# Narrow expert tiles: gate and up in four column groups, on branches of TensorE alone

## The chip, the cores and the metric

One core of a Trainium2 chip runs the whole kernel. The metric is the time of one execution on the device in microseconds; the time before is a median of 3 runs.

## The reference, cut to what matters

One decoder layer over 512 tokens of width 1024: a mixer (a Mamba-2 branch and a forgetting-attention branch between two large projections) and then a hierarchical mixture of 16 experts. The change touches the experts alone:

```python
def hierarchical_moe(h, w_rg, b_rg, w_re, b_re, w_gate, w_up, w_down):
    ...
    gates = (onehot_g[:, :, None] * w_group[:, None, :]).reshape(-1, N_EXPERTS).astype(t.dtype)
    out = jnp.zeros_like(t)
    for e in range(N_EXPERTS):
        hid = jax.nn.silu(t @ w_gate[e]) * (t @ w_up[e])
        out = out + gates[:, e:e + 1] * (hid @ w_down[e])
    return out.reshape(b, s, d)
```

Each token picks one group of four experts and two experts in it, so only two of its 16 gates are not zero. `w_gate` and `w_up` are 1024 x 512 for each expert, `w_down` 512 x 1024, all float32. With the inputs given, experts 0 to 15 get 31, 40, 95, 86, 27, 11, 40, 32, 91, 132, 170, 103, 25, 21, 59 and 61 tokens.

## The kernel before, in words

The mixer and the router fill the time up to about 576 us. Then, for each expert `e`, tokens are taken in tiles of `H` = 64 slots: `body(e, 0)` always, `body(e, 1)` under `tc.If(n_toks[e] > H)` (L1354) and `body(e, 2)` nested in it under `tc.If(n_toks[e] > 2 * H)` (L1356). With the counts above that makes 24 tiles. After the sixteen experts stand ten nested overflow blocks `over(t)` (from L1421), none of which runs with these inputs: all engines jump over them.

A tile goes through these steps. `tile_ranks` and `tile_tokens` (VectorE comparisons L1151, small TensorE matmuls L1156 and L1158, then a gather by GpSimd, L1161) make the list of the tile's tokens, two experts ahead, and fetch their rows; `x_columns` (L1181, four transposes) turns the rows; `up` (L1283 to 1289, matmul L1288) multiplies by gate and up; `hidden` (L1292, L1293) forms silu(gate) * up; `hidden_columns` (four transposes L1297, copy L1298) turns it; `down` (L1303) multiplies it by `w_down` one tile later; `add` (L1307, L1308) weighs the rows and scatter-adds them to memory.

In `up` the 64 tokens are the stationary side (128 x 64 weights of the array) and 512 columns of the expert's weights stream past. Gate goes to rows 0 to 63 of the PSUM bank, up to rows 64 to 127, eight steps of k each:

```python
for k in range(KT):
    for n, w in enumerate(strm.up(e, k)):
        nc.tensor.matmul(bank[n * H:(n + 1) * H], xT[:, ...], w, start=(k == 0), stop=(k == KT - 1))
```

A float32 matmul shows as two weight loads and two matmul records in the trace. Weights come in pieces of 1 MB on SyncE's queue into at least 18 buffers (`Experts.load`, `drop`, L355 to 376), some three experts' worth.

The order of TensorE, VectorE and ScalarE inside a body is the written one (`in_order`); around the bodies the scheduler places instructions itself, and moves some over an `If`. For a branch each engine loads the expert's count into a register (`values_load`, L1347; the load stands just ahead of the branch on all engines but SyncE, which loads all 16 at once) and its sequencer then compares and jumps over the code of the bodies that don't run.

Of the kernel before, what the change touches and what calls it, by code (L numbers as in the profile page):

```python
# [9 lines left out]
F32 = mybir.dt.float32  # L10
F32R = mybir.dt.float32r
BF16 = mybir.dt.bfloat16
I32 = mybir.dt.int32
# [4 lines left out]
P = 128  # L18
S = 512
D = 1024  # L20
NT = S // P
KT = D // P
FF = 512
NE = 16
# [4 lines left out]
UNIT = 512  # L29
EVAC = 400  # L30
DUE = 8, 4, 4
H = P // 2
INL = 3
MAXO = 10

# [72 lines left out]
def hybrid_layer(ctx: ExitStack, tc: tile.TileContext, A, out):  # L108
    nc = tc.nc

    cp = ctx.enter_context(tc.tile_pool(name="cp", bufs=1))
# [57 lines left out]
    ident = cp.tile([P, P], F32, name="ident")  # L169
# [67 lines left out]
    class Stream:  # L237
# [7 lines left out]
        def add(self, units, loads, parts):  # L245
            for n, part in enumerate(parts):
                self.parts.append((len(self.raws), n == len(parts) - 1) + part)
            self.raws.append((units, loads))
# [96 lines left out]
    class Experts:  # L345
# [18 lines left out]
        def up(self, e, k):  # L364

            assert self.nload >= 6 * e + 4
            return [self.piece(6 * e + 2 * (k // 4) + n)[:, k % 4 * FF:(k % 4 + 1) * FF] for n in range(2)]

        def down(self, e, k):
            assert self.nload >= 6 * e + 6  # L370
            return [self.piece(6 * e + 4 + k // 2)[:, k % 2 * D + n * 512:k % 2 * D + (n + 1) * 512]
                    for n in range(2)]
# [5 lines left out]
    ew = Experts([(wg_all[e], wu_all[e], wd_all[e]) for e in range(NE)], [])  # L378
# [25 lines left out]
    for j in range(4):  # L404
# [14 lines left out]
        for t, sc_ in enumerate((1, 0)):  # L419
            o = 8 * sc_ + 2 * j  # L420
# [142 lines left out]
    for g in range(4):  # L563
# [17 lines left out]
        for c in range(NT):  # L581
            nc.tensor.matmul(pt[:, c * P:(c + 1) * P], Bc.ap[:, c * P:(c + 1) * P], Cc.ap[:, c * P:(c + 1) * P],
                             start=True, stop=True)
# [14 lines left out]
        for c2 in range(2):  # L598
            pt = tr.get()
            for c in (2 * c2, 2 * c2 + 1):  # L600
                for t in range(2):
                    o = (c % 2) * 256 + t * P
# [96 lines left out]
    for j in range(4):  # L699
# [22 lines left out]
        for i in range(NT):  # L722
            w = (i + 1) * P
# [36 lines left out]
        o = FM.alloc(1)  # L760
# [81 lines left out]
    for j in range(8):  # L842
        for y in (ys[j], ya[j]):
            pt = proj(hT, KT)
            t = FM.alloc(1)
# [18 lines left out]
    def rtile(nm, shape, dt=F32):  # L864
        if dt is I32:
            return cp.tile(shape, dt, name=f"rt_{nm}")
        n = 1
        for d in shape[1:]:
            n *= d
        w = n if dt is F32 else -(-n // 2)  # L870
        a = rtc[0][:, rtc[1]:rtc[1] + w]
        if dt is not F32:
            a = a.bitcast(dt)[:, 0:n]
        rtc[1] += -(-w // 2) * 2
        for ax_ in range(len(shape) - 1, 1, -1):
            a = a.rearrange("p (a b) -> p a b", b=shape[ax_]) if ax_ == len(shape) - 1 else \
                a.rearrange("p (a b) c -> p a b c", b=shape[ax_])
        return a
# [8 lines left out]
    half = rtile("half", [P, 1])  # L887
    nc.vector.tensor_scalar(half, pcol, float(H), None, op0=ALU.is_ge)
    nc.vector.tensor_scalar(itb[:, 0:H], itf[:, 0:H], 1.0, None, op0=ALU.add)
    nc.vector.tensor_copy(itb[:, H:P], itb[:, 0:H])  # L890
    itbs = [itb] + [rtile(f"itb{t}", [P, P], BF16) for t in range(1, INL)]
    for t in range(1, INL):
        nc.vector.tensor_scalar(itbs[t], itb, float(t * H), None, op0=ALU.add)
    aux = rtile("aux", [P, NT, NE, 5], BF16)
# [82 lines left out]
    @contextmanager  # L977
    def in_order(engines):

        traced = nc.cur_bb.bb.instructions  # L980
        n, prev = len(traced), {}
        yield
        for ins in traced[n:]:
            if ins.engine in engines:
                if ins.engine in prev:
                    tc.add_manual_dep(ins, prev[ins.engine], mybir.DependencyInfo(
                        mybir.DependencyClass.NoSync, mybir.DependencyReason.DATA), reason="in_order")
                prev[ins.engine] = ins.name
# [60 lines left out]
    ET = mybir.EngineType  # L1049
# [60 lines left out]
    bgu, bys, bhid, bix = (banks[0], banks[1], banks[1]), [banks[2], banks[6]], banks[5], banks[7]  # L1110
    h2d2 = h2d.rearrange("s (h d) -> (s h) d", h=2)
    moed2 = moed.rearrange("s (h d) -> (s h) d", h=2)
    xgs, xTs, sgs, yos, ohs = {}, {}, [], [], []
# [12 lines left out]
    def setup_experts():  # L1126
# [6 lines left out]
        yos.extend(FM.alloc(1).ap for _ in range(2))  # L1133
        hidT.append(FM.alloc(1).v(4, H))
        for _ in range(3):
# [4 lines left out]
        ew.raws.append(xrc[1].ap)  # L1140
        ew.load()

    ixs = [[rtile(f"ix{e}{t}", [P, 1], I32) for t in range(INL)] for e in range(3)]
    gws = [[rtile(f"gw{e}{t}", [P, 1]) for t in range(INL)] for e in range(3)]
    ixl = [rtile(f"ixl{e}", [P, 1], I32) for e in range(2)]
    gwl = [rtile(f"gwl{e}", [P, 1]) for e in range(2)]
    rkx = rtile("rkx", [P, NT])

    def onehots(oh, ranks, slots):
# [3 lines left out]
    def tokens(oh, au, ix, gw, xg, n0=0, n1=5, at=128):  # L1153

        pi = bix[:, at + n0:at + n1]
        nc.tensor.matmul(pi, onesb, bigb[:, n0:n1], start=True, stop=False)  # L1156
        for c in range(NT):
            nc.tensor.matmul(pi, oh[:, c, :], au(c)[:, n0:n1], start=False, stop=(c == NT - 1))  # L1158
        if n0 == 0:
            nc.vector.tensor_scalar(ix, bix[:, at:at + 1], bix[:, at + 1:at + 2], half, op0=ALU.add, op1=ALU.add)  # L1160
            nc.gpsimd.indirect_dma_start(out=xg, out_offset=None, in_=h2d2,  # L1161
                                         in_offset=bass.IndirectOffsetOnAxis(ap=ix[:, 0:1], axis=0),
                                         bounds_check=2 * S - 1, oob_is_err=False)
        if n1 == 5:
            nc.vector.tensor_reduce(gw, bix[:, at + 2:at + 5], axis=AX.X, op=ALU.add)  # L1165

    def oh_of(e, t):
        return ohs[t if e or t == 2 else 3 + t]

    def tile_ranks(e, t):  # L1170
        onehots(oh_of(e, t), rk[:, :, e], itbs[t])

    def tile_tokens(e, t, n0=0, n1=5):
        tokens(oh_of(e, t), lambda c: aux[:, c, e, :], ixs[e % 3][t], gws[e % 3][t], xgs[e % 2, t], n0, n1,
               128 + 8 * (e % 2 * 3 + t))

    def x_columns(xg, xT):

        pt = tr.get()
        for b in range(4):  # L1180
            nc.tensor.transpose(pt[:, b * P:(b + 1) * P], xg[:, b * P:(b + 1) * P], ident)  # L1181
        nc.scalar.copy(xT, pt)  # L1182
# [21 lines left out]

    NB = S // H - INL
    cnt = rtile("cnt", [P, 16])
    cnti = rtile("cnti", [P, 17], I32)
# [20 lines left out]
    with in_order((ET.PE, ET.DVE, ET.Activation)):  # L1228
# [46 lines left out]
        for e, t in early:  # L1275
            tile_ranks(e, t)
            tile_tokens(e, t, 0, 2)
# [7 lines left out]
    def up(strm, e, xT, bank):  # L1285
        for k in range(KT):
            for n, w in enumerate(strm.up(e, k)):
                nc.tensor.matmul(bank[n * H:(n + 1) * H], xT[:, (2 * (k % 4) + k // 4) * H:(2 * (k % 4) + k // 4 + 1) * H],  # L1288
                                 w, start=(k == 0), stop=(k == KT - 1))

    def hidden(bank, sg):
        nc.scalar.activation(sg[H:P], bank[0:H], AF.Silu)  # L1292
        nc.vector.tensor_tensor(sg[H:P], sg[H:P], bank[H:P], op=ALU.mult)  # L1293

    def hidden_columns(sg):
        for t in range(4):
            nc.tensor.transpose(bhid[:, t * P:(t + 1) * P], sg[:, t * P:(t + 1) * P], ident)  # L1297
        nc.vector.tensor_copy(hidT[0], bhid.rearrange("p (k s) -> p k s", s=P)[:, :, H:P])  # L1298

    def down(strm, e, bank):  # L1300
# [11 lines left out]
    def body(e, t):  # L1312

        bank, by, yo, sg = bgu[t], bys[t % 2], yos[t % 2], sgs[t % 2]
        with in_order((ET.PE, ET.DVE, ET.Activation)):
            if t == 0:
                if e + 2 < NE:
                    for u in range(2):
                        tile_ranks(e + 2, u)
                tile_ranks(e, 2)  # L1320
            if t == 1:
                tile_tokens(e, 2)
            up(ew, e, xTs[e % 2, t], bank)
            if e == 0 and t == 0:
                for e_, t_ in early:
                    tile_tokens(e_, t_, 2, 5)
            hidden(bank, sg)
            nc.vector.tensor_copy(ixl[e % 2], ixs[e % 3][t])
            nc.vector.tensor_copy(gwl[e % 2], gws[e % 3][t])
            if t:  # L1330
                down(ew, e, by)
                add(by, yo, ixs[e % 3][t - 1], gws[e % 3][t - 1])
            elif e:
                down(ew, e - 1, by)
                add(by, yo, ixl[1 - e % 2], gwl[1 - e % 2])
                ew.drop(2)
            if t == 0 and e + 1 < NE:
                for u in range(2):
                    x_columns(xgs[1 - e % 2, u], xTs[1 - e % 2, u])
            if t == 1:  # L1340
                x_columns(xgs[e % 2, 2], xTs[e % 2, 2])
            hidden_columns(sg)
            if t == 0 and e + 2 < NE:
                for u in range(2):
                    tile_tokens(e + 2, u)

    n_toks = [nc.values_load(cnti[0:1, e:e + 1], min_val=0, max_val=S) for e in range(NE)]  # L1347
    n_over = nc.values_load(cnti[0:1, 16:17], min_val=0, max_val=MAXO)
    n_raw = len(ew.raws)
    assert n_raw >= 18  # L1350

# [6 lines left out]
        if e + 1 < NE:  # L1358
            ew.drop(4)
    down(ew, NE - 1, bys[0])  # L1360
    add(bys[0], yos[0], ixl[(NE - 1) % 2], gwl[(NE - 1) % 2])


    spare = [ew.piece(6 * (NE - 3) + n) for n in range(18)]
# [103 lines left out]
```

## Time and profile before

| what | value |
|---|---|
| median of 3 runs | 932.13 us (930.22 to 933.62) |
| the profiled execution's own time | 932.47 us |
| span of its trace | 930.6 us |
| mean granted clock of TensorE | 0.964 |
| TensorE busy | 842.8 us, 91% of the span |
| VectorE, ScalarE, GpSimd busy | 540.6, 309.6, 101.3 us |
| moved by the DMA engines | 194.88 MB, mean 209 GB/s |

The profile counts an engine as busy while a matmul, a copy or the like runs; register loads, branches and waits of the engine's sequencer are not in it, but they have rows of their own (engine names with a q at the end, as PEldq for TensorE's sequencer). [...] The share of DMA can come out a little over 1 in a short window.

### The profile page before, as it was taken

What the parts mean: (1) busy time and instruction counts of PE and PEld (TensorE: products, weight loads), DVE (VectorE), ACT (ScalarE), POOL (GpSimd) and SP (SyncE); (2) the same over time, 40 slices, a digit from 0 to 9 for tenths busy, and PEclk for the clock granted to TensorE, in tenths of its full rate; (3) what the DMA queues carried; (4) which work ended last, traced back from release to release, by engine and by line L of the source; (5) the groups of instructions that cost most, each with busy time, mean ns of one, the idle gap of its engine ahead of it and who ended that gap; (6) DMA issues with size and microseconds to landing.
All of it is one profiled execution on the core that took longest, in us unless ns stands there. A gap on an engine that the chain in (4) does not pass through costs nothing. (4 is left out here: it accounts for less than half of the span.)

```text
span 930.6 us, 11855 instructions
## 1 busy us (share of the span) xinstructions
PE 842.8 (91%) x4216; PEld 542.3 (58%) x4216; DVE 540.6 (58%) x1310; ACT 309.6 (33%) x558; POOL 101.3 (11%) x113
## 2 busy tenths in 40 slices
PE   2899989999999999999999995999999999999850
PEld 1678768887666677878888883433343333333320
DVE  6849879858876687977745784423333223122216
ACT  5438788444643432432233451101110010001100
POOL 1001000000000000000000011122222221122210
PEclk9899999999999999999999985999999999999985
DMA  9951457213122248795445289598799998459734
GB/s 288 340 147 52 152 173 191 87 40 103 46 69 72 91 140 268 222 302 160 147 143 186 106 305 398 211 385 296 247 391 386 385 381 287 145 192 314 278 71 180
DMA packets 137170, 194.88 MB, mean 209 GB/s; under 512 B 11819, under 2 KB 85723, under 8 KB 137073
## 3 DMA queue, kind: packets, MB, share of 16 engines
q1 hardware_dynamic: 127040, 174.81, 55.3%
q0 software_dynamic: 9584, 18.45, 7.6%
q8 instruction: 46, 0.75, 0.3%
q10 hardware_dynamic: 464, 0.58, 0.2%
q14 instruction: 36, 0.29, 0.1%
HBM read 189.04 MB, written 13.16 MB: 217 GB/s over the span
## 5 line engine op out<-in xcount | busy, mean ns | idle before, releaser
L398 PE MATMUL bank<-rm,rm 128*128 128x512 f32 x512 | 206.2, 407 | 0.4 <-ACT rm L431 0.4
L400 PE MATMUL bank<-rm,rm 128*128 128x512 f32 x512 | 205.8, 402 | 0.0
L399 PE MATMUL bank<-rm,rm 128*128 128x512 f32 x512 | 204.8, 400 | 0.2 <-DVE rm L433 0.2
L1288 PE MATMUL bank<-fm,fm 128*64 128x512 f32 x408 | 123.8, 601 | 4.4 <-issue 2.0
L1288 PE MATMUL bank<-bm,fm 128*64 128x512 f32 x360 | 118.4, 597 | 1.6 <-PEq L1356 0.4
L234 DVE TENSOR_TENSOR rm<-fm,rm 128x1024 fp32r<-128x1024 f32 (+1 forms) x76 | 87.6, 1163 | 42.9 <-ACT rm L233 27.3
L398 PEld LDWEIGHTS bank<-rm,rm 128*128 128x128 f32 x512 | 97.8, 192 | 21.9 <-issue 3.1
L399 PEld LDWEIGHTS bank<-rm,rm 128*128 128x128 f32 x512 | 97.4, 190 | 21.5 <-issue 2.1
L400 PEld LDWEIGHTS bank<-rm,rm 128*128 128x128 f32 x512 | 97.1, 190 | 20.8 <-issue 2.3
L1293 DVE TENSOR_TENSOR bm<-bm,bank 64x512 f32<-64x512 f32 x24 | 16.6, 692 | 152.4 <-ACT bm L1292 143.4
L233 ACT CAST rm<-fm 128x1024 fp32r<-128x1024 f32 (+1 forms) x76 | 75.2, 1007 | 79.5 <-PE bank L399 59.5
L1292 ACT ACTIVATE bm<-bank 64x512 f32<-64x512 f32 x24 | 14.1, 588 | 198.8 <-PE bank L1288 198.8
L1288 PEld LDWEIGHTS bank<-fm,fm 128*64 128x64 f32 x408 | 37.9, 138 | 59.3 <-issue 58.4
L1303 PE MATMUL bank<-bm,fm 128*64 128x512 f32 x256 | 65.2, 593 | 0.7 <-DVEq L1354 0.7
L1288 PEld LDWEIGHTS bank<-bm,fm 128*64 128x64 f32 x360 | 34.7, 137 | 47.7 <-issue 46.8
L390 DVE SCALAR_TENSOR_TENSOR fm<-fm,cact,fm 128x256 f32<-128x256 f32 x112 | 51.2, 480 | 1.8
L1182 ACT COPY fm<-bank 128x512 f32<-128x512 f32 x38 | 20.9, 588 | 85.8 <-PE bank L1181 85.7
L1307 DVE SCALAR_TENSOR_TENSOR fm<-bank,fm,fm 128x512 f32<-128x512 f32 x24 | 18.0, 750 | 47.8 <-PE bank L1303 42.8
L1001 PE MATMUL bank<-rm,rm 128*128 128x512 f32 x192 | 44.2, 391 | 0.3 <-ACT fm L846 0.3
L1161 POOL DMA_INDIRECT bm<-h2d,rt_ix x38 | 39.0, 1027 | 38.9 <-DVE fm L1165 18.2
L1303 PEld LDWEIGHTS bank<-bm,fm 128*64 128x64 f32 x256 | 22.1, 137 | 35.3 <-issue 34.4
L1308 POOL DMA_INDIRECT moed<-fm,rt_ixl x16 | 25.5, 1596 | 152.2 <-DVE fm L1307 152.2
(314 smaller groups left out, 1101.7 us busy)
## 6 DMA issues: line engine op xcount, KB each, us to landing
bm<-in_w_down SPq DMA_DIRECT2D x22, 1024.0 KB
fm<-in_w_in SPq DMA_DIRECT2D x36, 512.0 KB
fm<-in_w_gate SPq DMA_DIRECT2D x17, 1024.0 KB
fm<-in_w_mod SPq DMA_DIRECT2D x16, 1024.0 KB
fm<-in_w_up SPq DMA_DIRECT2D x16, 1024.0 KB
bm<-in_w_up SPq DMA_DIRECT2D x16, 1024.0 KB
bm<-in_w_gate SPq DMA_DIRECT2D x15, 1024.0 KB
fm<-in_w_down SPq DMA_DIRECT2D x10, 1024.0 KB
```

The lines of the kernel that those rows point to most:

```text
L233: ins = nc.scalar.copy(hi, src)
L234: nc.vector.tensor_tensor(lo, src, hi.bitcast(F32), op=ALU.subtract)
L390: nc.vector.scalar_tensor_tensor(acc, r, cact[:, k:k + 1], acc, op0=ALU.mult, op1=ALU.add)
L398: nc.tensor.matmul(pt, whi[:, k, :], ah.ap, start=(k == 0), stop=False)
L399: nc.tensor.matmul(pt, whi[:, k, :], al.ap, start=False, stop=False)
L400: nc.tensor.matmul(pt, wlo[:, k, :], ah.ap, start=False, stop=(k == nk - 1))
L1001: nc.tensor.matmul(wps[i][hf], sta.ap[:, tsl], mov.ap[:, hf * 512:(hf + 1) * 512], start=(k == 0 and sta is mh and mov is wh), stop=(k == ...
L1161: nc.gpsimd.indirect_dma_start(out=xg, out_offset=None, in_=h2d2, in_offset=bass.IndirectOffsetOnAxis(ap=ix[:, 0:1], axis=0), bounds_check ...
L1182: nc.scalar.copy(xT, pt)
L1288: nc.tensor.matmul(bank[n * H:(n + 1) * H], xT[:, (2 * (k % 4) + k // 4) * H:(2 * (k % 4) + k // 4 + 1) * H], w, start=(k == 0), stop=(k = ...
L1303: nc.tensor.matmul(bank[n * H:(n + 1) * H], hidT[0][:, k, :], w, start=(k == 0), stop=(k == 3))
L1308: nc.gpsimd.indirect_dma_start(out=moed2, in_=yo, in_offset=None, compute_op=ALU.add, out_offset=bass.IndirectOffsetOnAxis(ap=ix[:, 0:1], ...
```

## The change

Expert tiles with at most `Q` = 32 tokens take another form of two steps. `up_few` uses only 32 of the 64 stationary columns, and splits gate and up by halves of their 512 columns: four blocks of 32 rows of the bank, each with 256 columns, 32 matmuls of 128 x 32 by 256 in place of 16 of 128 x 64 by 512. `turn_few` follows that layout: four float32 matmuls against 32 columns of the identity in place of four transposes. `by_width` chooses at run time, by an `If` and `Else` on TensorE alone, from a count that is loaded on TensorE (`n_pe`). Tiles (0, 0) and (0, 2) keep the old form without a branch. With the inputs given nine tiles hold at most 32 tokens and have the branch: the first tiles of e4, e5, e7, e12 and e13, the second of e2, e3 and e8, the third of e9. The lists of slots and gate weights (`ixs`, `gws`, `ixl`, `gwl`) become slices of one tile each, with a place of its own for every expert instead of two or three that are used in turn.

```diff
-H = P // 2
+H, Q = P // 2, P // 4
...
-    ixs = [[rtile(f"ix{e}{t}", [P, 1], I32) for t in range(INL)] for e in range(3)]
-    gws = [[rtile(f"gw{e}{t}", [P, 1]) for t in range(INL)] for e in range(3)]
-    ixl = [rtile(f"ixl{e}", [P, 1], I32) for e in range(2)]
-    gwl = [rtile(f"gwl{e}", [P, 1]) for e in range(2)]
+
+    ixa, gwa = cp.tile([P, NE, INL + 1], I32, name="ixa"), cp.tile([P, NE, INL + 1], F32, name="gwa")
+    ixs, gws = ([[a[:, e, t:t + 1] for t in range(INL)] for e in range(NE)] for a in (ixa, gwa))
+    ixl, gwl = ([a[:, e, INL:INL + 1] for e in range(NE)] for a in (ixa, gwa))
...
-        tokens(oh_of(e, t), lambda c: aux[:, c, e, :], ixs[e % 3][t], gws[e % 3][t], xgs[e % 2, t], n0, n1,
+        tokens(oh_of(e, t), lambda c: aux[:, c, e, :], ixs[e][t], gws[e][t], xgs[e % 2, t], n0, n1,
...
+    def up_few(strm, e, xT, bank):
+        for k in range(KT):
+            at = (2 * (k % 4) + k // 4) * H
+            for n, w in enumerate(strm.up(e, k)):
+                for hf in range(2):
+                    o = n * H + hf * Q
+                    nc.tensor.matmul(bank[o:o + Q, 0:256], xT[:, at:at + Q], w[:, hf * 256:(hf + 1) * 256],
+                                     start=(k == 0), stop=(k == KT - 1), tile_position=(0, o))
...
-    def hidden_columns(sg):
+    def by_width(is_few, few, other, *args):
+        if is_few is None:
+            return other(*args)
+        with tc.If(is_few) as arm:
+            with in_order((ET.PE,)):
+                few(*args)
+        with arm.Else():
+            with in_order((ET.PE,)):
+                other(*args)
+
+    def turn_few(sg):
+        for t in range(4):
+            o = H + t // 2 * Q
+            nc.tensor.matmul(bhid[:, t * P + H:t * P + H + Q], sg[:, t % 2 * P:(t % 2 + 1) * P], ident[:, o:o + Q],
+                             start=True, stop=True)
+
+    def turn(sg):
         for t in range(4):
             nc.tensor.transpose(bhid[:, t * P:(t + 1) * P], sg[:, t * P:(t + 1) * P], ident)
+
+    def hidden_columns(sg, is_few=None):
+        by_width(is_few, turn_few, turn, sg)
...
+        is_few = None if (e, t) in wide else n_pe[e] <= t * H + Q
...
-            up(ew, e, xTs[e % 2, t], bank)
+            by_width(is_few, up_few, up, ew, e, xTs[e % 2, t], bank)
...
-            nc.vector.tensor_copy(ixl[e % 2], ixs[e % 3][t])
-            nc.vector.tensor_copy(gwl[e % 2], gws[e % 3][t])
+            nc.vector.tensor_copy(ixl[e], ixs[e][t])
+            nc.vector.tensor_copy(gwl[e], gws[e][t])
             if t:
                 down(ew, e, by)
-                add(by, yo, ixs[e % 3][t - 1], gws[e % 3][t - 1])
+                add(by, yo, ixs[e][t - 1], gws[e][t - 1])
             elif e:
                 down(ew, e - 1, by)
-                add(by, yo, ixl[1 - e % 2], gwl[1 - e % 2])
+                add(by, yo, ixl[e - 1], gwl[e - 1])
...
-            hidden_columns(sg)
+            hidden_columns(sg, is_few)
...
+    wide = (0, 0), (0, 2)
     n_toks = [nc.values_load(cnti[0:1, e:e + 1], min_val=0, max_val=S) for e in range(NE)]
     n_over = nc.values_load(cnti[0:1, 16:17], min_val=0, max_val=MAXO)
+    n_pe = [nc.values_load(cnti[0:1, e:e + 1], engines=(ET.PE,), min_val=0, max_val=S) for e in range(NE)]
```

The program of TensorE grows from 3949 to 5039 rows. Counted in its compiled form, the code that L1354's branch (L1389 now) jumps over, bodies 1 and 2, is 231 instructions before and 533 to 535 now (383 for expert 0); for the inner branch, body 2 alone, it is 106 before and 256 now.

TensorE at expert 0's first gate matmul, the difference from before; L1181 are `x_columns`, L1383 is `n_pe`, L1288 is `up`:

```order
+L1181 MATMUL bank_65<-ident,bm_3742 128x128 x4
+L1181 MATMUL bank_64<-ident,bm_3742 128x128 x4
+L1383 TENSOR_LOAD rt_cnti
+L1383 ISA x2
+L1383 TENSOR_LOAD rt_cnti
...
+L1383 ISA x2
 L1288 MATMUL bank_61<-fm_79,fm_81 64x512
 L1288 MATMUL bank_61<-fm_69,fm_81 64x512
```

Sixteen register loads, each with two small instructions, now stand in a row between the transposes and the first gate matmul.

TensorE around the branch of e4 before (L1156 and L1158 are the lists of e6, L1288 the gate and up matmuls of e5):

```order
2576 L1158 LDWEIGHTS fm_74
2577 L1158 MATMUL bank_68<-fm_80,fm_74 128x5
2578 L1288 MATMUL bank_61<-fm_73,fm_75 64x512
2579 L1288 MATMUL bank_61<-bm_3762,fm_75 64x512
2580 L1288 MATMUL bank_61<-fm_73,fm_75 64x512
2581 L1288 MATMUL bank_61<-bm_3762,fm_75 64x512
2582 L1347 TENSOR_LOAD rt_cnti
2583 L1354 COMPARE_AND_BRANCH
2584 L1156 LDWEIGHTS fm_80
2585 L1156 MATMUL bank_68<-fm_80 128x5
```

and in the changed kernel, the same place (L1381 is the load, L1389 the branch, L1311 the choice by width, L1301 `up_few`):

```order
2860 L1158 LDWEIGHTS fm_74
2861 L1158 MATMUL bank_68<-fm_80,fm_74 128x5
2862 L1381 TENSOR_LOAD rt_cnti
2863 L1389 COMPARE_AND_BRANCH
2864 L1156 LDWEIGHTS fm_80
2865 L1156 MATMUL bank_68<-fm_80 128x5
...
2874 L1311 COMPARE_AND_BRANCH
2875 L1301 MATMUL bank_62<-bm_3747,fm_81 32x256 x2
2876 L1301 MATMUL bank_62<-bm_3748,fm_81 32x256 x2
2877 L1301 MATMUL bank_62<-bm_3747,fm_81 32x256 x2
```

Gate and up matmuls of the next expert no longer stand ahead of the branch; from e3 on all of them come behind it, inside their own choice by width.

## Rows read from the trace of the kernel before

**Rows 1.** The page: busy time of TensorE, its share of the span, instructions.

```profile
PE 842.8 (91%) x4216; PEld 542.3 (58%) x4216; DVE 540.6 (58%) x1310; ACT 309.6 (33%) x558; POOL 101.3 (11%) x113
```

**Rows 2.** Windows: from:to, us, busy us of each engine, granted clock, DMA share, GB/s.

```profile
600.00:625.00 25.00, 24.45 (x134) 10.34 (x131) 8.51 (x39) 2.73 (x5) 8.32 (x7) 1.00 1.05 383
...
700.00:725.00 25.00, 24.18 (x129) 10.81 (x126) 6.41 (x26) 3.09 (x6) 4.67 (x5) 1.00 1.05 386
...
800.00:825.00 25.00, 24.71 (x123) 9.36 (x120) 5.84 (x16) 2.40 (x5) 3.43 (x3) 1.00 0.69 209
```

**Rows 3.** Timeline of TensorE: start, us, operation; gate (fm) and up (bm) records.

```profile
650.56 0.59 PE L1288 MATMUL bank<-fm,fm 128*64 128x512 f32 x1
650.57 0.59 PE L1288 MATMUL bank<-bm,fm 128*64 128x512 f32 x1
650.99 0.59 PE L1288 MATMUL bank<-fm,fm 128*64 128x512 f32 x1
```

**Rows 4.** The costliest groups: busy us, mean ns of one, idle before.

```profile
L1288 PE MATMUL bank<-fm,fm 128*64 128x512 f32 x408 | 123.8, 601 | 4.4 <-issue 2.0
L1288 PE MATMUL bank<-bm,fm 128*64 128x512 f32 x360 | 118.4, 597 | 1.6 <-PEq L1356 0.4
...
L1288 PEld LDWEIGHTS bank<-fm,fm 128*64 128x64 f32 x408 | 37.9, 138 | 59.3 <-issue 58.4
```

**Rows 5.** Groups of lines, 546 to 552 us: the router's float32 matmuls.

```profile
L1040 PEld LDWEIGHTS bank<-wr,fm 128*128 128x128 f32 x43 | 5.0, 192 | 0.0
L1040 PE MATMUL bank<-wr,fm 128*128 128x20 f32 x43 | 4.9, 262 | 0.0
```

**Rows 6.** Timeline of TensorE around the branch of e4, 681.8 to 683.5 us.

```profile
681.85 0.60 PE L1297 MATMUL bank<-ident,bm 128*128 128x128 f32 x4
682.28 0.17 PE L1156 MATMUL bank<-fm 128*128 128x5 bf16 x1
682.31 0.24 PE L1158 MATMUL bank<-fm,fm 128*128 128x5 bf16 x4
683.22 0.17 PE L1156 MATMUL bank<-fm 128*128 128x5 bf16 x1 [0.67 <-DVE fm L1298]
```

**Rows 7.** Count loads (min/median/max ns, first and last start), and expert 0's first matmuls.

```profile
L1347 SPq TENSOR_LOAD <-rt_cnti x16: 261/262/490, 572.7 to 581.7; - x16
...
L1347 PEldq TENSOR_LOAD <-rt_cnti x16: 297/300/490, 590.8 to 891.2; - x16
...
578.58 1.97 PE L1288 MATMUL bank<-fm,fm 128*64 128x512 f32 x4
```

**Rows 8.** The branch over bodies 1 and 2, on TensorE's sequencer (min/median/max ns).

```profile
L1354 PEldq COMPARE_BRANCH  x16: 70/316/452, 591.4 to 891.6; - x16
```

**Rows 9.** The branch over the ten overflow blocks, TensorE and VectorE.

```profile
L1421 PEldq COMPARE_BRANCH  x1: 3393/3393/3393, 895.0 to 895.0; - x1
...
L1421 DVEq COMPARE_BRANCH  x1: 56/56/56, 899.8 to 899.8; - x1
...
L1421 DVEq EVENT_SEMAPHORE  x1: 21/21/21, 902.7 to 902.7; - x1
```

**Rows 10.** Queues' packets and MB: whole span (x46, x36), and 894.9 to 900 us.

```profile
q8 instruction: 46, 0.75, 0.3%
...
q14 instruction: 36, 0.29, 0.1%
...
q8 instruction: 2, 0.03, 2.3%
```

**Rows 11.** Windows around an idle stretch in the mixer, columns as in rows 2.

```profile
122.00:125.50 3.50, 0.10 (x1) 0.00 (x0) 2.13 (x4) 3.50 (x7) 0.00 (x0) 1.00 0.90 277
...
126.50:129.90 3.40, 3.40 (x11) 2.67 (x10) 2.94 (x8) 3.27 (x8) 0.14 (x1) 0.50 0.29 77
129.90:133.00 3.10, 3.10 (x16) 2.64 (x15) 1.87 (x4) 2.27 (x5) 0.00 (x0) 1.00 0.00 0
```

More of the change, by code (lines that the diff above doesn't have):

```diff
@@ L1360, in hybrid_layer @@
     down(ew, NE - 1, bys[0])
-    add(bys[0], yos[0], ixl[(NE - 1) % 2], gwl[(NE - 1) % 2])
+    add(bys[0], yos[0], ixl[NE - 1], gwl[NE - 1])
     spare = [ew.piece(6 * (NE - 3) + n) for n in range(18)]
```

## Prediction, made before the change was run

> **What bounds the kernel now.** I read the page first. TensorE is busy for 842.8 us of the span, 91% [rows 1]; the chain that ended last is no help inside the expert stage, since it names mostly the scatter at the end. So I cut the expert stage (about 576 to 898 us) into windows: TensorE is busy for 24.45 us of 25 early in it, and for 24.18 us while the DMA engines are full at 1.05 [rows 2]. A microsecond that TensorE saves there is a microsecond of the kernel, and so is one that it stands still. The sum is made against the profiled execution, 932.5 us, which lies 0.3 us above the median of the three runs, 932.1. A change of about 0.3% (2.8 us) is what a measurement here can tell from none.
>
> **What one tile costs, and what a narrow one would.** Follow the starts in the timeline: a gate record and an up record start together, and the next two 0.43 us later [rows 3]. The 768 records over 24 tiles [rows 4] are 32 for a tile, 16 pairs, so a tile's gate and up take 16 x 0.43 = 6.9 us. Each record shows 0.59 us of its own [rows 4], so the two column halves of the array do run side by side. With the router's counts of these inputs 9 of the 24 tiles hold at most 32 tokens and take the new branch: e2 and e3 in their second tile, e4, e5, e7, e8's second, e9's third, e12 and e13.
>
> A narrow tile issues 32 matmuls of 256 columns, 64 records. Bounds: if four column groups run side by side, 16 steps of half of 0.43 us make 3.4 us; if only two do, 6.9 us; if none, 13.8 us. Between the first two stands the rate at which small records follow each other, 64 instead of 32 each with a weight load: 20-column fp32 records with 128-column weights, 43 in 4.9 us of busy time, come one in 0.112 us [rows 5], which would make 64 x 0.112 = 7.2 us; bf16 records of five columns, four in 0.24 us, come one in 0.06 us [rows 6], 3.8 us. I take 3.8: the new weights are 32 columns wide, and a weight load falls from 192 to 138 ns as the weights narrow from 128 to 64 columns [rows 4, 5]. Gain 9 x (6.9 - 3.8) = **-28 us**, between -31 and +3 by the small-record bounds.
>
> The turn of a narrow tile's hidden block replaces four transposes by four fp32 matmuls with 128-column weights: 8 records of 0.112 us [rows 5], 0.9 us, for the 0.43 us between the start of those transposes and of what follows them [rows 6], that is 9 x 0.47 = **+4 us** (0 if they hide as the transposes do, 6 if nothing does). Copies of indices and gate weights into longer-lived tiles are the same instructions: 0; more names mean fewer waits, but TensorE's idle rows show none for them.
>
> **The sixteen loads.** All of n_pe is read on TensorE in one block, which the order puts between expert 0's transposes and its first gate matmul. SyncE reads the same 16 numbers from 572.7 to 581.7 us, 0.6 us apart [rows 7]; a TensorE load takes 300 ns against SyncE's 262 [rows 7], so 16 x 0.6 = 9.6 us, of which some 0.9 us lie beside the transposes still queued. The first gate matmul starts at 578.58 [rows 7] and nothing behind it can pass: **+9 us** (5 by the load alone, 11 at most).
>
> **New branches.** A branch not taken takes 70 ns, the middle one 316, the longest 452 [rows 8]. Most of the 48 new pairs lie behind queued matmuls. Twelve stand where nothing is queued, since expert e's gate matmuls, one to five of which stood before the previous expert's branch, now come behind it: 12 x 0.4, and 6 turns lose about 0.4 us of hoisted work: **+7 us** (4 to 12).
>
> So far: -28 + 4 + 9 + 7 = -8, 924.5 us.
>
> **The jump that got longer.** This decides the sign. Twelve experts have no second tile, and TensorE's sequencer jumps over bodies 1 and 2 at once: 231 instructions before, 533 to 535 now, as both widths of every matmul stand there. What do jumps cost? Those of 231 cost at most 452 ns [rows 8]. The only long one of TensorE, 1270 instructions over the ten overflow blocks, holds its sequencer for 3393 ns [rows 9]. VectorE's, about 256 instructions, shows its compare at 899.8 and the next instruction at 902.7 [rows 9], 2.9 us, though its wait there is for its own work, long done.
>
> The fetch packets say why: TensorE's queue moved 46 packets of 16 KB, the others' 36 of 8 KB [rows 10]. Laid along the stream, one comes for each 256 instructions that TensorE passes (128 on the others). In those blocks TensorE's 231 are 0.9 block and cheap, 1270 are 5 and dear, VectorE's 256 are 2.0 and dear. Around TensorE's long jump only two packets move in five microseconds [rows 10], one of them for the target: not several blocks ahead, so a target two blocks on isn't loaded. The new jumps are 533/256 = 2.08 blocks: every one lands beyond the block after the current one.
>
> [...]
>
> Who waits? Before the branch of e4 the timeline shows the small matmuls of the next expert's lists waiting 0.67 us for VectorE [rows 6]: the queue is empty when the sequencer jumps. The same holds for e5, e6, e7, e12 and e13: 6 x (3.4 - 0.35) = +18. e1 hides a little: +2.5. e14 and e15 build no lists, and a down block and transposes are queued: 0. e0's jump is shorter (383), and the loads have already been paid. Sum **+21** (0 if no jump stalls, 25 with all of them, up to 2 us more each while the DMA engines are full, since a packet must then queue).
>
> Where the landing lies within some tens of instructions of the next block's end (e4, e7, e12, the exit of e8), that block isn't there yet either: **+6** (0 to 17).
>
> **The clock.** [...] Six of them: **+10 us** (0 to 17).
>
> Sum: -8 + 21 + 6 + 10 = +29, that is 961.5; I say **962 us**.
>
> **Rivals.**
> 1. *The jump isn't dear* (the other side): TensorE's stream holds more blocks ahead than its packets let me see, and a 2.08-block jump costs 0.3 to 0.45 us as 0.9 does. For it: only one long jump is on record, over five blocks, and VectorE's blocks are smaller. Against it: one packet per block passed, and two around the long jump. Then the three terms from jump, landing and clock fall away: about 924, 915 at best if the loads hide and small records are at their lower bound, 931 at worst. It decides from a cost per jump of about 0.8 us down: the sum's -8 is used up by some nine exposed events of 0.9 us. Chance 0.16.
> 2. *Four groups gain nothing*: weight loads or records come one in 0.11 us, or the array runs only two groups at once. Then -28 becomes about +1 and the sum with stalls is 990. For it, 0.112 us [rows 5] is the nearest fp32 row; against it, those weights are four times as wide. Chance 0.15.
> 3. *The transfers become the bound.* They run at 1.05 [rows 2] through the middle of the stage. But from 800 us on the share is 0.69 [rows 2]: there the loads wait for TensorE to free their buffers, not the reverse, so a slower TensorE only gives them more time, and one faster by 28 us over the whole stage uses up little. It would take rival 1 first, then give about 930: inside its 0.16.
> 4. *The narrow branch is hardly taken or paid*: queues refill in the shadow of long tiles, stalls halve, and the kernel ends within 2.8 us of before. It needs the stall terms to come to about 8 instead of 37. Chance 0.05.
>
> **The numbers.** Forecast 0.64, its own range 942 to 978: on the 924.5 the jumps almost alone, +18, up to all three terms at their upper ends with some queueing of packets, +54. Rival 1 adds 0.16 below and rival 2 0.15 above. The range from 924 to 990 takes the forecast whole, half of rival 1 and half of rival 2. Faster by more than 0.3%: rival 1 nearly whole, 0.15. Same: 0.05. Slower: 0.80.
>
> **What would show it.** In the profile after: TensorE's If branch at 3 us or more, twelve times at most and in e4, e5, e6, e7, e12, e13 for sure; narrow tiles' gate and up at 3.4 to 4 us, with records of about a third of 0.59; sixteen loads in a row and expert 0's first gate matmul at about 587 to 588; granted clock below 1.00 in windows after the stalls. If the branch stays below 0.5 us everywhere, the forecast is wrong and rival 1 holds; if the narrow blocks take 6.5 us or more, rival 2 does.

## The result and the profile after

| | before | after |
|---|---|---|
| median | 932.65 us (4 runs, 930.2 to 933.6) | 991.49 us (4 runs, 988.6 to 996.1) |
| ratio | | 1.064, 95% interval 1.0592 to 1.0687 |
| span of the profiled execution | 930.6 us | 994.3 us |
| mean granted clock | 0.964 | 0.912 |

The change makes the kernel 6.4% slower. The forecast was 962 and the range ended at 990, 1.5 us short. What follows is counted on the spans of the two profiled executions, which lie 63.7 us apart; the one of the changed kernel, 996.1 us, is the slowest of its four runs, 4.6 over the median. First the page of the changed kernel: TensorE's busy time, and its instruction queue.

```profile
PE 831.1 (84%) x4540; PEld 549.0 (55%) x4540; DVE 539.4 (54%) x1310; ACT 309.8 (31%) x558; POOL 101.4 (10%) x113
...
q8 instruction: 70, 1.15, 0.5%
```

TensorE is busy for 11.7 us less than in [rows 1] although the run is longer: work went away, idle time came. It fetched 70 blocks of code where it fetched 46 [rows 10]; a block is what one packet of q8 brings, 16 KB by the row above (1.15 MB in 70). In the mixer of the kernel before, 20 of them start from 45.66 to 550.51 us, and between the first and the last stand 4910 of TensorE's matmul and weight-load records, one packet for some 258. The windows of the stage, columns as in [rows 2]:

```profile
600.00:625.00 25.00, 21.83 (x104) 8.05 (x104) 6.19 (x26) 2.94 (x6) 3.62 (x3) 0.86 0.56 196
700.00:725.00 25.00, 17.37 (x126) 7.99 (x120) 4.87 (x22) 1.76 (x3) 3.67 (x3) 0.73 0.95 347
800.00:825.00 25.00, 23.57 (x181) 10.70 (x179) 8.01 (x30) 2.84 (x5) 7.23 (x6) 1.00 0.69 224
```

From 700 us TensorE is busy for 17.37 us of 25 where it was for 24.18 [rows 2], and its granted clock, a share of its full rate, is at 0.73. From 800 to 825 us, where experts with several tiles are worked on and no jump is long, the stage is nearly as it was. The branches' own rows (shortest, middle and longest in ns) name the cause; L1389 was L1354 [rows 8], L1311 is the choice by width, L1456 was L1421 [rows 9], L1383 the sixteen loads:

```profile
L1389 PEldq COMPARE_BRANCH  x16: 77/4172/6577, 609.9 to 952.5; - x16
...
L1311 PEldq COMPARE_BRANCH  x64: 64/200/3262, 599.8 to 949.7; - x64
...
L1456 PEldq COMPARE_BRANCH  x1: 4807/4807/4807, 958.6 to 958.6; - x1
...
L1383 PEldq TENSOR_LOAD <-rt_cnti x16: 297/299/490, 576.9 to 587.5; - x16
```

The branch over bodies 1 and 2 has a middle value of 4172 ns instead of 316. The choice by width is cheap, 200 ns, but once 3262. The timeline at e4's branch, the place of [rows 6]:

```profile
692.81 0.17 PE L1156 MATMUL bank<-fm 128*128 128x5 bf16 x1 [0.67 <-DVE gwa L1165]
692.83 0.24 PE L1158 MATMUL bank<-fm,fm 128*128 128x5 bf16 x4
699.71 0.64 PE L1301 MATMUL bank<-bm,fm 128*32 128x256 f32 x2 [6.63 <-PEq L1389]
699.72 0.64 PE L1301 MATMUL bank<-fm,fm 128*32 128x256 f32 x2
700.10 0.67 PE L1301 MATMUL bank<-bm,fm 128*32 128x256 f32 x2
```

After the lists TensorE stands for 6.63 us, released by its own sequencer at L1389, and then runs at half rate (granted clock 0.50 from 696.19 to 703.01 us): the next four narrow records start 0.39 to 0.43 us later. Undisturbed, in e3's second tile, they start 0.21 us apart:

```profile
666.94 0.39 PE L1301 MATMUL bank<-fm,fm 128*32 128x256 f32 x2
666.95 0.39 PE L1301 MATMUL bank<-bm,fm 128*32 128x256 f32 x2
667.16 0.39 PE L1301 MATMUL bank<-fm,fm 128*32 128x256 f32 x2
```

So four groups do run side by side; that tile takes 3.6 us from 664.76 to 668.35. All nine long jumps as windows (the first, two of the middle, the last, and the sum; from e1's to e15's):

```profile
628.50:632.40 3.90, 0.00 (x0) 0.00 (x0) 1.22 (x8) 0.00 (x0) 1.80 (x2) 0.86 0.70 247
...
711.60:717.70 6.10, 0.00 (x0) 0.00 (x0) 1.20 (x8) 0.00 (x0) 2.00 (x2) 0.64 1.05 382
...
752.80:762.80 10.00, 0.00 (x0) 0.00 (x0) 1.94 (x12) 0.00 (x0) 2.02 (x2) 0.57 1.00 351
...
952.60:957.50 4.90, 2.15 (x12) 0.77 (x8) 1.08 (x2) 1.00 (x1) 1.58 (x1) 1.00 0.75 225
sum 54.10, PE 5.12 PEld 2.37 DVE 10.71 ACT 2.08 POOL 18.50; mean PE 0.57 PEld 0.26 DVE 1.19 ACT 0.23 POOL 2.06
```

TensorE is busy for 5.1 of these 54.1 us. e7's window, 10 us, holds two stalls: the jump, and right behind it 3.26 us at L1311 from 759.56, for the block after the landing, whose packet starts at 760.31. And the stretches of the stage with a granted clock of 0.50, ten of them: behind the loads, behind e0's turn, behind the gather that is shown below, behind e5's jump, and the sum of the ten; below them the one of the kernel before:

```profile
576.00:593.79 17.79, 7.25 (x22) 3.02 (x22) 4.06 (x20) 2.77 (x5) 0.00 (x0) 0.50 0.35 132
610.86:617.68 6.82, 5.89 (x14) 1.40 (x16) 2.43 (x12) 0.54 (x1) 1.00 (x1) 0.50 0.93 311
...
675.71:685.95 10.24, 8.49 (x68) 5.70 (x72) 1.26 (x5) 0.59 (x1) 0.67 (x1) 0.50 0.86 277
...
713.25:723.50 10.25, 5.10 (x12) 1.68 (x14) 0.74 (x4) 0.00 (x0) 0.66 (x1) 0.50 0.93 345
...
sum 106.53, PE 55.40 PEld 23.96 DVE 14.41 ACT 4.93 POOL 7.43; mean PE 5.54 PEld 2.40 DVE 1.44 ACT 0.49 POOL 0.74
...
576.00:580.46 4.46, 4.02 (x14) 2.08 (x16) 0.00 (x0) 2.34 (x3) 0.00 (x0) 0.50 1.06 384
```

55.4 us of work at half the full rate, 27.7 of them lost; before, the stage had 4.0 us of such work (576 to 580.46 us), 2.0 lost. Two more waits, the first gate matmul behind the sixteen loads, and a transpose behind a gather:

```profile
588.40 1.98 PE L1288 MATMUL bank<-fm,fm 128*64 128x512 f32 x4 [10.49 <-issue]
...
676.80 1.09 PE L1181 MATMUL bank<-ident,bm 128*128 128x128 f32 x4 [4.79 <-DMA bm<-h2d,ixa]
```

The account of the 63.7 us: long jumps and e7's second stall 49.0 idle, less some 0.4 us each that nine branches cost before [rows 8], **+45.4**; clock **+25.7**; loads 588.40 - 578.58 = **+9.8** [rows 7]; the gather **+4.8**; one run out of code in e13's gate and up (3.20 us of idle at 908.78, no jump in it) **+3.2**; the narrow form itself **-24.7** (never_narrow, below). Together 64.2. The terms are known to a few us only, so part of so close a sum is luck: on the two profiled spans never_narrow lies 20.2 us above the changed kernel, not 24.7; of what the nine branches took before, most lay behind queued matmuls; and the account has no term for the lists' matmuls (L1156), which wait 11.9 us where they waited 6.8 before.

### The profile page after: what moved, and what is told of

Read it like the earlier page. It is cut to its first block, busy times and chain, and to the rows that moved or that the text cites. A ratio compares the mean times of both kernels' runs of the same rounds, so it can differ in the third digit from the quotient of the medians.

```text
span 994.3 us, 12629 instructions
## 1 busy us (share of the span) xinstructions
PE 831.1 (84%) x4540; PEld 549.0 (55%) x4540; DVE 539.4 (54%) x1310; ACT 309.8 (31%) x558; POOL 101.4 (10%) x113
## 3 DMA queue, kind: packets, MB, share of 16 engines
q8 instruction: 70, 1.15, 0.5%
## 5 line engine op out<-in xcount | busy, mean ns | idle before, releaser
L398 PE MATMUL bank<-rm,rm 128*128 128x512 f32 x512 | 205.6, 405 | 0.4 <-ACT rm L431 0.4
L400 PE MATMUL bank<-rm,rm 128*128 128x512 f32 x512 | 205.1, 401 | 0.0
L399 PE MATMUL bank<-rm,rm 128*128 128x512 f32 x512 | 204.6, 400 | 0.2 <-DVE rm L433 0.2
L1288 PE MATMUL bank<-fm,fm 128*64 128x512 f32 x264 | 87.5, 657 | 20.8 <-issue 11.7
L1288 PE MATMUL bank<-bm,fm 128*64 128x512 f32 x216 | 72.7, 618 | 17.5 <-issue 10.4
L1335 PE MATMUL bank<-bm,fm 128*64 128x512 f32 x256 | 65.9, 660 | 9.3 <-PEq L1389 7.4
L1340 POOL DMA_INDIRECT moed<-fm,ixa x24 | 38.4, 1602 | 259.5 <-DVE fm L1339 240.1
L1151 DVE TENSOR_SCALAR fm<-fm 128x128 bf16<-128x128 bf16 x192 | 36.7, 262 | 48.2 <-PEq L1389 35.7
L1288 PEld LDWEIGHTS bank<-fm,fm 128*64 128x64 f32 x264 | 27.0, 151 | 59.5 <-issue 59.3
L1301 PE MATMUL bank<-bm,fm 128*32 128x256 f32 x288 | 31.9, 520 | 24.6 <-PEq L1389 20.7
L1339 DVE SCALAR_TENSOR_TENSOR fm<-bank,gwa,fm 128x512 f32<-128x512 f32 x24 | 18.0, 750 | 58.2 <-PE bank L1335 58.2
L1288 PEld LDWEIGHTS bank<-bm,fm 128*64 128x64 f32 x216 | 21.6, 142 | 46.4 <-issue 45.3
L1335 PEld LDWEIGHTS bank<-bm,fm 128*64 128x64 f32 x256 | 19.8, 150 | 49.0 <-issue 47.4
```

Source lines behind the costliest of these rows:

```text
L398: nc.tensor.matmul(pt, whi[:, k, :], ah.ap, start=(k == 0), stop=False)
L399: nc.tensor.matmul(pt, whi[:, k, :], al.ap, start=False, stop=False)
L400: nc.tensor.matmul(pt, wlo[:, k, :], ah.ap, start=False, stop=(k == nk - 1))
L1151: nc.vector.tensor_scalar(oh[:, c, :], slots, ranks[:, c:c + 1], None, op0=ALU.is_equal)
L1301: nc.tensor.matmul(bank[o:o + Q, 0:256], xT[:, at:at + Q], w[:, hf * 256:(hf + 1) * 256], start=(k == 0), stop=(k == KT - 1), tile_positio ...
L1335: nc.tensor.matmul(bank[n * H:(n + 1) * H], hidT[0][:, k, :], w, start=(k == 0), stop=(k == 3))
```

## The experiments

Theory A: a jump to a block of code that isn't there waits for a fetch, and that fetch queues behind the weights' transfers. The rivals: a far jump costs 6 us by itself; the length, not the block, decides; the choice by width is at fault.

**no_weight_loads**, the changed kernel, in `Experts.load`:

```diff
-                nc.sync.dma_start(self.piece(self.nload).rearrange("p (a b) -> p a b", b=n), src)
+                if self.nload < 18 or nk == 0:
+                    nc.sync.dma_start(self.piece(self.nload).rearrange("p (a b) -> p a b", b=n), src)
```

> The changed kernel without the weight transfers after the first 18 pieces of 1 MB (the later experts compute with the weights that are there, so their results are not the reference's). Nothing else is changed, so all jumps are as long as in the changed kernel. Theory A, the fetch of a jump's target waits behind weight transfers in the DMA engines: the long jumps, 5.7 to 6.6 us in the changed kernel, fall to about 3.4 us as the one long jump of the kernel before, and the time falls by some 20 us (jumps) and a part of the 27 us that the clock costs, to 950 to 970. Rival B, a far jump costs about 6 us whatever the DMA engines do: the jumps stay at 5.5 us or more and the time stays over 980.

Measured: 940.4 us (one run), 51 less and below the expected 950 to 970. The branch over bodies 1 and 2 is L1390 here:

```profile
L1390 PEldq COMPARE_BRANCH  x16: 77/3371/5767, 612.3 to 895.4; - x16
```

e4 fell from 6.0 to 3.3 us, e5 from 6.1 to 3.4, e7 from 6.6 to 3.6, e12 from 6.3 to 4.1, e13 from 5.7 to 3.5. The packets tell where the time went: at e4 in the changed kernel the packet starts 3.7 us after the branch (693.24, 696.93), here 1.0 us after (686.71, 687.73); from the packet's start to the end of the branch it is 2.3 us in both. Theory A holds for the size, the rival of a fixed 6 us falls. The gain is larger than expected: TensorE's waits behind this branch fall from 43.7 to 19.3 us, half clock loses 15.3 us of work where it lost 27.7, and other waits get shorter too, which was not taken apart. Two stay dear without weights: e6 at 4.8, where two packets follow each other and the target's is the second, and e15 at 5.8.

**never_narrow**, the changed kernel, in `body`:

```diff
-        is_few = None if (e, t) in wide else n_pe[e] <= t * H + Q
+        is_few = None if (e, t) in wide else n_pe[e] <= t * H
```

> The changed kernel with the narrow branch never taken (the comparison asks for no tokens in the tile): all loads, branches and both widths' code stay, every tile computes the wide form. It shows what the narrow form gives in the changed kernel itself. If the stalls are the code's and the narrow form's gain is real, 991.5 + 9 x 3.1 = 1019, between 1010 and 1026, with the long jumps at 5 us or more as before. Rival, the narrow tiles' gain is lost in waits for blocks and gathers: 991 to 1003.

Measured: 1016.2 us (one run), L1389 at 77/4030/6329 ns. The loads, branches and doubled code cost 83 us over the kernel before; the narrow form gives 24.7 of them back, 2.7 a tile, against four runs that reach from 988.6 to 996.1. The rival falls.

**padded_before**, the kernel before:

```diff
                 body(e, 2)
+                for _ in range(PAD.get(e, 0)):
+                    nc.tensor.matmul(bix[:, 300:305], onesb, bigb[:, 0:5], start=True, stop=True)
```

> The kernel before, with small matmuls that never run put behind body 2, so that the jump over bodies 1 and 2 grows by a chosen length for some experts: 362 instructions for e4, e5, e7, e12, e13, e14 and e15, 514 for e6, 284 for e1, 234 for the others. By the layout of the program the landing is one block of 256 instructions further for e0, e1, e4, e5 and e15, and two blocks further for e6, e7, e12, e13 and e14. Block theory: e6, e7, e12, e13 and e14 stall for 3.4 to 6.6 us each, e4, e5 and e15 cost below 0.5 us although their jump is just as long, and the time grows by 20 to 35 us. Rival, the length alone decides (some instructions ahead are loaded, wherever the block ends): e4, e5 and e15 cost the same as e7, e12 and e13. Rival, the jump isn't the cause at all but the choice by width: no branch costs over 0.5 us and the time stays at 932.

Measured: 976.9 us (one run). No narrow form, no new branch, no early load, only code that never runs, and 43 us are gone (the kernel before beside it: 934.3). The branch, and the matmuls behind it for e4, e5, e6 and e7, in the timeline of this kernel:

```profile
L1355 PEldq COMPARE_BRANCH  x16: 70/2006/6712, 591.0 to 934.1; - x16
...
677.08 1.08 PE L1288 MATMUL bank<-fm,fm 128*64 128x512 f32 x1 [4.41 <-PEq L1355]
...
697.42 1.12 PE L1288 MATMUL bank<-fm,fm 128*64 128x512 f32 x2 [5.46 <-PEq L1355]
...
719.55 1.12 PE L1288 MATMUL bank<-bm,fm 128*64 128x512 f32 x2 [5.46 <-PEq L1355]
...
735.55 0.61 PE L1288 MATMUL bank<-fm,fm 128*64 128x512 f32 x1
```

e4, e5 and e7 jump over the same 362 instructions (359 without three labels, as the 231 were counted): the branch takes 6.2 and 6.0 us for the first two, of which queued matmuls cover some, and 0.43 for e7. So the length alone doesn't decide, and the choice by width, which this kernel lacks, isn't needed for the stall. My list of who would stall was wrong for five of them (e1, e4, e5 and e15 stalled, e7 didn't): I had put the block borders where the program's first instruction would have them. Moved by 42 instructions, an offset that I fitted afterwards to the branches of this and four other profiles (before, after, no_weight_loads, narrow_fixed), the borders sort nearly all taken branches by one rule, dear beyond the next block and cheap within it; five exceptions remain, e5 here among them, all of them dear where the rule says cheap.

The traces give the borders without a fit. Twelve times in eight of the profiles TensorE waits in straight code, with no jump at that place (loads_alone, below, shows two), and each wait ends 2.2 to 2.7 us after one of its code packets starts; counted in the compiled form, the first late instruction stands at the same place of the 256 all twelve times. By that, an estimate from these twelve waits, the borders lie as if 62 instructions stood ahead of the program's first, not 42. Then e5 here lands on the first instruction of the block after the next and is no exception. Of the 100 jumps over bodies 1 and 2 in ten of the profiles (lists_alone was not counted), all 33 that land beyond the next block take 3.3 us or more. Of the other 67, 58 take under 0.5 us, and the nine dear ones all leave a block within 89 instructions of its start, which the next pair is about. The instructions alone don't decide: e7 here stands 35 behind a border and costs 0.43 us, but its target's packet had started 3.35 us before the branch.

**narrow_fixed**, then **fixed_shifted**, the changed kernel with the width chosen when the program is built (no loads, no branch; `CN` holds the sixteen counts):

```diff
-        is_few = None if (e, t) in wide else n_pe[e] <= t * H + Q
+        is_few = (e, t) not in wide and t * H < CN[e] <= t * H + Q
...
+        return (few if is_few else other)(*args)
```

and for the second also

```diff
                 body(e, 2)
+                for _ in range(18 if e == 6 else 0):
+                    nc.tensor.matmul(bix[:, 300:305], onesb, bigb[:, 0:5], start=True, stop=True)
```

> The narrow form for the same nine tiles, but chosen when the program is built, from the counts of these inputs: no count loads on TensorE, no choice by width at run time, jumps at 231 instructions. It shows what the narrow form is worth by itself. Expected from the silu to silu steps of the changed kernel, 3.2 us less for each undisturbed narrow tile: 9 x 3.2 = 29 less, some 5 given back where the third tile's gather is late behind a narrow second tile, so 903 to 911. Rival, the small matmuls hide nothing and the transfers or the gathers take the gain: 925 or more.

Measured: 927.2 us, ratio 0.992 (0.9899 to 0.994). Undisturbed narrow tiles do gain 3.4 us each from one tile's silu to the next, but e7 and e13 stall at jumps of 232 instructions:

```profile
710.51 1.09 PE L1288 MATMUL bank<-bm,fm 128*64 128x512 f32 x1 [6.60 <-PEq L1382]
...
864.70 1.09 PE L1288 MATMUL bank<-bm,fm 128*64 128x512 f32 x1 [6.49 <-PEq L1382]
```

Their targets are in the next block by the borders above, so dear beyond it and cheap within it can't be the whole. Both branches stand shortly behind a border, 61 and 53 instructions by the borders above; the 35 to 40 and the 69 to 77 of the next expectation are counted from the fitted ones.

> The narrow form chosen when the program is built, as in narrow_fixed, with 18 small matmuls that never run put behind body 2 of e6. They change no work; they only shift all later code by 36 instructions. In narrow_fixed the branches of e7 and e13 stood some 35 to 40 instructions behind the start of a block and stalled for 6.1 and 6.0 us although their jumps are only 232 instructions; the shift puts them 69 to 77 instructions behind it. Theory, the next block is asked for on entering a block and takes about 5 us to come while weights stream, so a jump into it soon after the entry waits: e7 and e13 now cost below 1 us, and the time is 927 - 2 x 6 - some 5 of clock = 907 to 915. Rival, these two experts' branches wait for something else (a late load, a gather): they stall as before, and the time stays at 925 to 930.

Measured: 919.7 us, ratio 0.9843 (0.9807 to 0.988), 7.5 less than narrow_fixed for 36 instructions that never run. The same two places:

```profile
704.43 0.61 PE L1288 MATMUL bank<-bm,fm 128*64 128x512 f32 x1 [0.86 <-PEq L1382]
...
854.08 1.08 PE L1288 MATMUL bank<-bm,fm 128*64 128x512 f32 x1 [3.00 <-PEq L1382]
```

e7's stall is gone, e13's went from 6.0 to 2.5 us (it stands at 89 instructions, e7 at 97). The rival falls. So the runs bear out that who jumps into the next block too early waits for the rest of its coming: for e13 its packet starts 3.7 us after the branch in narrow_fixed and with the branch here. That it is asked for on entering the block ahead of it is an estimate from these places and times and was not shown by itself. The time is 4.7 us above the top of what I expected: a part of e13's stall is left, and 2.4 us of idle without a jump in e7's gate and up. This version is faster than both kernels, but its widths are those of these inputs.

**loads_alone**, the kernel before with the line `n_pe = ...` and no use of it.

> The kernel before with the 16 count loads on TensorE and nothing else; no instruction uses them. They stand in a row between expert 0's transposes and its first gate matmul, as in the changed kernel. Expected from the changed kernel's own rows: 9.8 us later first matmul and 1.8 us of half clock behind the idle stretch, 932.6 + 11.6 = 944, between 941 and 946. Rival, the loads only shift idle time that is found again later (the weights' transfers get a lead of 10 us): below 936.

Measured: 959.0 us, ratio 1.0257 (1.0215 to 1.0299), 15 more than expected. The first gate matmul is late by 10.1 us, as expected:

```profile
588.67 5.04 PE L1288 MATMUL bank<-fm,fm 128*64 128x512 f32 x11 [10.46 <-issue]
...
702.10 1.86 PE L1288 MATMUL bank<-fm,fm 128*64 128x512 f32 x3 [5.34 <-DMA bm<-in_w_up]
...
737.72 1.01 PE L1288 MATMUL bank<-bm,fm 128*64 128x512 f32 x1 [3.59 <-issue]
```

The rest is new waits, 5.34 us at e5, 3.59 us amid a tile, and 3.4 and 3.1 us at the branches of e1 and e14, and the half clock behind them. The loads are 48 instructions, so they moved all later code against the borders; e1 and e14 now branch shortly behind one, 67 and 68 instructions. The view puts the 5.34 us down to a weight piece; but the late instruction is the first of a block, and a code packet starts 2.35 us ahead of it (699.75), as 2.38 us ahead of the 3.59 us wait's (735.34), so this too reads as a wait for code.

**first_tiles_only** and **first_tiles_spread**, the changed kernel:

```diff
-        is_few = None if (e, t) in wide else n_pe[e] <= t * H + Q
+        is_few = None if t or e == 0 else n_pe[e] <= Q
```

and for the second the load of `n_pe[e]` moved into the loop ahead of `body(e, 0)`.

> The changed kernel with the choice by width in first tiles alone (e4, e5, e7, e12 and e13 are narrow); later tiles keep the old form, so the jump over bodies 1 and 2 is 231 instructions again. The 16 count loads stay in a row. Block theory: no jump costs over 0.5 us, the granted clock stays at 1.00 after expert 0, and the time is 932.5 + 11.5 for the loads and the clock behind them - 5 x 3.2 = 928, between 923 and 932. Rival, the choice by width itself breaks the queue: jumps at L1389 stay at 3 us or more and the time stays over 960.

Measured: 968.5 us, ratio 1.0363 (1.0304 to 1.0422), 40 above what I expected. L1389 itself was mended (77/334/2164 ns), but

```profile
L1311 PEldq COMPARE_BRANCH  x40: 64/212/5604, 601.7 to 924.7; - x40
...
PE bank L1181 <- DMA bm<-h2d,ixa: 13.8, 4, 5.2
...
PE bank L1301 <- issue: 6.7, 2, 4.1
```

the waits moved: 5.6 us at the choice by width right behind e5's jump (it begins at 709.74, and the packet it waits for starts at 713.00), 6.7 us amid narrow tiles with no jump, and 13.8 us for gathers at transposes, 5.2 of which are the first gather, which the kernel before waits for as well. The jump over bodies 1 and 2 is short again, but the block behind it still comes late, its packet 3.26 us after the choice by width begins, and there are more blocks to fetch than before: 55 packets instead of 46. Both of my theories fell as written.

> first_tiles_only with each expert's count loaded on TensorE in the loop over experts, so that only one load stands ahead of expert 0's first gate matmul and the others are spread over the first experts' work. Theory: the first gate matmul starts some 9 us earlier and at less half clock, 968.5 - 11 = 957.5, plus or minus some 8 us since every later block boundary lies elsewhere; waits for blocks of code remain, so it stays above 945. Rival, the waits of first_tiles_only come from the loads (everything is late against the weights' transfers): below 940.

Measured: 956.3 us, ratio 1.0254 (1.0217 to 1.0291), 12 less. Expert 0's first gate matmul starts at 577.09 us, with no wait:

```profile
577.09 5.09 PE L1288 MATMUL bank<-fm,fm 128*64 128x512 f32 x17
```

The loads' own price is as it was put; the waits for code stay (L1311 up to 5657 ns).

**lists_alone**, the kernel before with `ixa` and `gwa`.

> The kernel before with the lists of slots and gate weights as slices of one tile with a place for every expert, and nothing else of the change. Expected no difference, 930 to 936: TensorE waits for VectorE's list instructions in the same places. Rival, one tile for all makes waits that separate tiles did not have (TensorE's small matmuls wait 10.6 us for that tile in the changed kernel, 20 times): 936 to 942.

Measured: 933.7 us, ratio 1.0003 (0.9984 to 1.0021): no difference.

## Why the prediction was wrong

The side and the mechanism were right, the size was not: 962 forecast, 991.5 measured. Two terms were sized too low, the longer jump and the clock. By its own steps:

- **Narrow tiles**, -28 + 4 = -24: measured -24.7, by one run. Four groups run side by side, 3.6 us a tile where 3.8 was put, though each record shows 0.39 us and not a third of 0.59. Rival 2 is out.
- **The sixteen loads**, +9: measured +9.8, and again +10.1 alone. Their move of all later code was not in the sum.
- **New branches**, +7: the choice by width shows 200 ns in the middle, mostly behind queued work. The account has no term for it; the lists' longer waits (11.9 us against 6.8) and the half clock behind e0's turn, where no jump is long, are of the kind that this term was for.
- **The longer jump**, +21: measured +42.0. This is the step that failed first, by price more than by number. The six jumps of e4, e5, e6, e7, e12 and e13 cost 35.0 where 18 was put. Their price of 3.4 us came from the one long jump of [rows 9], at the end of the kernel, where few transfers run (0.41 MB from 894.9 to 900 us, 81 GB/s, against 386 in [rows 2] from 700 us on); the same jump costs 6.0 to 6.6 us at e4 to e7, and 3.3 to 4.8 without weight transfers. I had written "up to 2 us more" for that, and left it out of the sum although [rows 2] show the share at 1.05 in the middle of the stage. By number: e1 cost 3.9 us for the 2.5 that was put, and e14 and e15, put at nothing, left TensorE idle for 1.5 and 2.8 us of their 4.5 and 5.0, since the queued work was only some 3.0 and 2.2 us.
- **The landing**, +6: measured +3.4, e7's second stall. The 3.2 us that e13's gate and up ran out of code come on top.
- **The clock**, +10: measured +25.7. I had priced six stalls at 1.7 us of lost work each, half of the 3.4 us at a granted clock of 0.50 that follow a nearly idle stretch of 3.5 us in [rows 11]. The seven stretches at 0.50 behind jumps lost 1.4 to 3.9 us each, 16.9 together, and three that I had not counted lost 10.8 more: 3.6 behind the loads, 2.9 behind e0's turn, 4.2 behind the gather; 2.0 of it was there before.
- **Not foreseen:** +4.8 for the gather of e3's third tile. Its list is made at 664.56 and its rows are wanted behind a short tile and a down block, at 672.0; before, the same two stood at 646.43 and 657.10. e3 has no third tile that would use them.
- **The range and the counts.** The top of the forecast's own range, 978, was said to hold all three terms at their upper ends, +54; these ends, 25, 17 and 17, add to 59 before any queueing, and with "up to 2 us more" for six jumps to 71, that is 995.5. The bounds written down for the terms held the result; neither this range nor the wider one to 990 did. "Twelve experts have no second tile" should be ten, as the list of names beside it has it (e0 and the nine that jump far); and 43 in 4.9 us are one in 0.114 us, not 0.112, which changes nothing.

padded_before bears out the reading by blocks, with 6.2 us at e4, whose target lies beyond the next block by the borders above, and 0.43 at e7, whose target lies within it. It isn't the whole: in narrow_fixed a target in the next block stalled as well, for 6.1 us.

## What to carry to other kernels

Code that never ran had a price here where TensorE's sequencer had to jump over it, 43 us in padded_before, and the same 362 instructions cost 6.2 us at e4 and 0.43 at e7: count the instructions between a branch and its target and see in which block of 256 each lies (in the mixer one code packet came for some 258 of TensorE's records), and take the price of a jump from a stretch with the same DMA traffic, not from a quiet one (6.0 to 6.6 us at e4 to e7, 3.4 at the end of the kernel before). Doubling code for a rare case cost more here than the case gave, 83 us for 24.7. A test that moves code also moves the borders (36 instructions were worth 7.5 us in fixed_shifted), so small differences between versions with branches need the rows of the branches beside the times.

## What the runs showed of the hardware that was not expected

- 36 instructions that never run changed the time from 927.2 to 919.7 us, and a stall of 6.1 us at one branch to 0.3.
- The next block of code came late without any jump: TensorE stood for 3.59 us amid a tile in loads_alone and for 3.20 us in the changed kernel, with nothing else to wait for. That these two are waits for code was not tried by itself; it is read from the packets, which start 2.38 and 2.34 us ahead, and from the late instruction, which is the first of a block both times, as in ten other such waits.
- e15's jump costs 5.8 us without weight transfers and 5.0 with them. Without them its branch stands 9 instructions behind a border, and as at e6 the target's packet (2.45 us after the branch) follows another (1.69); why neither starts sooner stays open.
